# TensorE's order between search and attention written by hand, search counts queued behind chosen evictions, and a third staging buffer for weights

## The chip, the cores and the metric

The kernel runs on one core of one Trainium2 chip. The metric is device time of one execution in microseconds (us). Five engines work side by side, each through its own instructions in a fixed order: TensorE (PE in the profile, with PEld for its weight loads), VectorE (DVE), ScalarE (ACT), GpSimd (POOL) and SyncE (SP), which here only issues DMA transfers. An engine whose next instruction has to wait holds up everything behind it.

## The reference

Two layers (DEPTH = 2) over 1024 positions of width 1024, in float32. Cut to what matters:

```
for l in range(DEPTH):
    h = rmsnorm(x, g_pre[l]) * (1 + scale) + shift
    p = h @ w_in[l]
    u_val, u_gate, g_conv, c_q, c_kv, k_idx, w_idx, g_attn = split(p)
    y_conv = conformer_conv(u_val, u_gate, ...) * silu(g_conv)
    y_attn = dsa_attention(c_q, c_kv, k_idx, w_idx, ...) * silu(g_attn)
    y = concatenate([y_conv, y_attn]) @ w_out[l]
    x = x + gate * rmsnorm(y, g_post[l])

conformer_conv: a = u_val * sigmoid(u_gate); causal depthwise conv, width 31;
                layernorm over 512 channels; silu; @ w_pw2
dsa_attention:  score[t, s] = sum_h w[t, h] * relu(q_idx[t, h] . k_idx[s])
                keep the 256 best keys of each query (causal), add a relative bias,
                softmax over them, times the latent values (8 heads), @ w_uv
```

## The kernel before

The work of a layer runs in five parts: latents (the narrow columns of `w_in`), the indexer (the scores), a **middle**, the attention, and the output projection. Every float32 product that needs precision is three TensorE products of a high and a low half (`mm3`, lines 85 to 89), so matrices are first split by `load_w` (line 91): a DMA brings a third of the matrix into a staging tile `raw` (two such buffers), ScalarE writes the high half (line 107), GpSimd or VectorE the low half (line 108).

The middle is what the change rewrites. It holds six kinds of work.

- `u_proj` (line 583): eight blocks of 48 products of 512 columns, for the two inputs of the convolution. Blocks 1 to 3 are spread between the index products by `tc.issue_after(marks[...])`; blocks 4 to 7 follow them. VectorE evicts every second block (line 601), and a finished pair goes to DRAM (`ad`, line 603).
- `conv` (line 606): eight blocks `c_block(q)`. Each reads back a rearranged piece of `ad` into `at` (line 616, pieces of 128 bytes), loads four weight tiles `wt` of 512 KB (line 626; five buffers of tag `t4`), makes 32 small products (64 instructions in the trace), and is evicted by VectorE into `An` (line 637).
- `gate_proj` (line 677): eight projections of 48 products, whose results ScalarE evicts through Silu (line 688), four into `yc` and four into `ya`.
- `conv_norm` (line 644): layer norm of `An` by `bn_stats` and `bn_aggr` on VectorE, two tiny products and 32 scalings (line 671).
- `pw2` (line 704): for each of four position groups `zt` transposes, Silu on ScalarE, a split into `silh` and `sill`, 48 products `pw`, and four multiplications into `yc` on VectorE (`gated`, line 738).
- `topk` (line 472): a bitwise binary search for each query's 256th best score, 15 and then 16 steps. Each step counts, in six score tiles of 384 to 1024 columns, how many scores lie below a candidate: three tiles on VectorE (line 528), three on ScalarE (line 525), and GpSimd makes the next candidate. Then, tile by tile, the kept keys are marked (lines 570 to 580, the **selection**).

Attention (line 753) goes over four pairs of heads and, in each, over four chunks of 256 queries, c = 0 to 3 (the last pair in the order 3, 1, 2, 0). Chunk c needs the selection of score tiles 2c-2 and 2c-1 only, chunk 0 needs none. `split` (line 854) then splits `yc` and `ya` for the output projection.

The order is a planner's: the program text gives priorities, a simulated time line picks what each engine runs next, and the result is a fixed order per engine. `EARLY`, `STEPS` and the calls in lines 983 to 1034 set the text's order. SP's transfers are ordered the same way, so one that waits for its data holds up those behind it.

## Time and profile before

| | |
|---|---|
| median of 3 runs | 1253.68 us (1253.31 to 1253.84) |
| the profiled execution | 1254.51 us, of which 1252.8 us is its span |
| TensorE busy / mean granted clock | 1188.3 us (95%) / 0.983 |
| VectorE, ScalarE, GpSimd busy | 915.3, 688.1, 628.0 us |
| DMA | 128.10 MB, mean 102 GB/s |

The stage tables below give, for a stretch of the span, the busy time of each engine, then the granted TensorE clock as a share of full speed, the share of time in which the DMA engines were busy, and GB/s. A stretch of TensorE at clock 0.50 runs its products at half speed. A busy TensorE is not proof of full speed, since the ends of pipelined products are modelled; idle time of it is real.

### The profile page before, as it was taken

Reading aid. Unit: us, or ns where it says so; the run is one execution under the profiler, and the core shown is the slowest. Engines: PE = TensorE matmul, PEld = TensorE weight load, DVE = VectorE, ACT = ScalarE, POOL = GpSimd, SP = SyncE. Lnnn points to the kernel's source line nnn. Section 1 sums busy time; section 2 is a strip of 40 time slices with the busy share of each in tenths; the row PEclk is TensorE's granted clock in tenths of the full one; section 3 lists DMA queues with packets and bytes.
Section 4 is the critical chain, followed back from the end, with each engine's and each line's share of the span. In section 5 each row is a group of like instructions: output and inputs, shape, how many; then the busy total and the mean of one; then the engine's idle time right before and its main releaser. Section 6 shows DMA issues by size and latency. Waiting matters only on the chain. (4 is left out here: it accounts for less than half of the span.)

```text
span 1252.8 us, 23059 instructions
## 1 busy us (share of the span) xinstructions
PE 1188.3 (95%) x7832; PEld 974.9 (78%) x7832; DVE 915.3 (73%) x2239; ACT 688.1 (55%) x1580; POOL 628.0 (50%) x1222
## 2 busy tenths in 40 slices
PE   6999999898998999999999999989979899999998
PEld 3888888557886777789988888866768677777998
DVE  3667899999777667757686579989985866677214
ACT  3645768667626556522355466877682465564221
POOL 3441146447536457855585202554673465588222
PEclk9999999899999999999999999989989899999999
DMA  9411266771010000137751123767111100012215
GB/s 360 144 51 34 52 206 209 243 250 52 11 43 21 9 9 26 52 108 267 241 202 53 44 51 107 233 209 211 55 32 28 34 10 5 5 54 74 74 35 185
DMA packets 90854, 128.10 MB, mean 102 GB/s; under 512 B 41320, under 2 KB 68464, under 8 KB 90736
## 3 DMA queue, kind: packets, MB, share of 16 engines
q1 hardware_dynamic: 90736, 126.63, 31.6%
q8 instruction: 62, 1.02, 0.3%
q14 instruction: 56, 0.46, 0.1%
HBM read 114.01 MB, written 12.59 MB: 101 GB/s over the span
## 5 line engine op out<-in xcount | busy, mean ns | idle before, releaser
L528 DVE TENSOR_SCALAR_CACHE_REDUCE jv<-pl,cand 128x768 int16<-128x768 uint16 (+1 forms) x186 | 187.8, 1009 | 17.7 <-DVE jv L528 6.6
L525 ACT ACTIVATE ja<-pl,cand 128x896 int8<-128x896 uint16 (+1 forms) x186 | 153.8, 827 | 40.6 <-POOL cand L535 34.8
L803 ACT ACTIVATE p<-p,mx 128x128 f32<-128x128 f32 (+7 forms) x128 | 98.8, 772 | 55.1 <-DVE mx L800 53.1
L805 POOL TENSOR_SCALAR p<-p,ri 128x128 f32<-128x128 f32 (+7 forms) x128 | 99.8, 784 | 43.8 <-DVE ri L804 43.5
L108 POOL TENSOR_TENSOR wul<-raw,wuh 128x342 fp32r<-128x342 f32 (+1 forms) x48 | 48.6, 1022 | 132.1 <-ACT wuh L107 116.9
L89 PE MATMUL o<-woh,yl 128*128 128x256 f32 x384 | 108.7, 283 | 2.1 <-POOL yl L861 2.1
L87 PE MATMUL o<-woh,yh 128*128 128x256 f32 x384 | 109.4, 286 | 0.5 <-DVE yrr L903 0.5
L88 PE MATMUL o<-wol,yh 128*128 128x256 f32 x384 | 108.5, 283 | 0.0
L87 PE MATMUL g<-hT,wgh 128*128 128x512 f32 x256 | 103.3, 404 | 2.6 <-ACT ya L688 2.2
L89 PE MATMUL g<-hT,wgl 128*128 128x512 f32 x256 | 102.3, 399 | 0.0
L88 PE MATMUL g<-hT,wgh 128*128 128x512 f32 x256 | 101.6, 397 | 0.0
L87 PE MATMUL u<-hT,wuh 128*128 128x512 f32 x256 | 100.8, 394 | 0.0
L88 PE MATMUL u<-hT,wuh 128*128 128x512 f32 x256 | 100.0, 391 | 0.0
L89 PE MATMUL u<-hT,wul 128*128 128x512 f32 x256 | 99.9, 390 | 0.0
L817 PE MATMUL pt<-ident,p 128*128 128x128 f32 x576 | 94.6, 278 | 2.4 <-ACT pt L822 1.7
L790 POOL TENSOR_TENSOR p<-tb,score 128x256 f32<-128x256 f32 x96 | 71.2, 749 | 48.2 <-PE pt L817 46.1
L843 PE MATMUL av<-pt,v 128*64 128x256 f32 (+1 forms) x640 | 93.3, 368 | 0.0
L461 DVE SCALAR_TENSOR_TENSOR score<-relu,widx,score 128x384 f32<-128x384 f32 (+2 forms) x84 | 79.2, 976 | 18.4 <-ACT relu L453 17.5
L817 PEld LDWEIGHTS pt<-ident,p 128*128 128x128 f32 x576 | 67.4, 140 | 25.5 <-issue 10.9
L822 ACT ACTIVATE pt<-pt 128x512 f32<-128x512 f32 (+2 forms) x96 | 50.2, 523 | 64.4 <-PE pt L817 63.8
L453 ACT ACTIVATE relu<-ixs 128x512 f32<-128x512 f32 (+2 forms) x140 | 66.4, 522 | 34.5 <-PE ixs L447 34.1
L447 PE MATMUL ixs<-ix 128*128 128x512 f32 (+2 forms) x320 | 76.3, 356 | 0.4 <-DVE ix L436 0.4
(302 smaller groups left out, 3463.6 us busy)
## 6 DMA issues: line engine op xcount, KB each, us to landing
wt<-in_wl_dram SPq DMA_DIRECT2D x64, 512.0 KB, 5.1
wa<-in_w_mod_dram SPq DMA_DIRECT2D x32, 512.0 KB, 5.2
raw<-in_w_in_dram SPq DMA_DIRECT2D x64, 171.0 KB, 2.5
wa<-in_w_ada_dram SPq DMA_DIRECT2D x16, 512.0 KB, 9.8
raw<-in_w_out_dram SPq DMA_DIRECT2D x32, 171.0 KB, 2.4
raw<-in_w_in_dram SPq DMA_DIRECT2D x32, 170.0 KB, 2.6
ad<-A SPq DMA_DIRECT2D x8, 512.0 KB, 3.3
at<-ad SPq DMA_DIRECT2D x16, 256.0 KB, 6.5
```

What stands on the lines that cost most here:

```text
L87: T.matmul(o, ah, bh, start=first, stop=False)
L88: T.matmul(o, ah, bl, start=False, stop=False)
L89: return T.matmul(o, al, bh, start=False, stop=last)
L447: mark = T.matmul(o[:, :c1 - c0], s_[:, 128 * i:128 * i + 128], ix[:, kk, c0:c1], start=kk == 0, stop=kk == 1)
L461: V.scalar_tensor_tensor(acc, r[:, :w], wc, acc, op0=OP.mult, op1=OP.add)
L525: S.activation(ja[:, :wid(j)], src, AF.Sign, scale=-1.0, bias=col(cand, c), accum_out=col(ct_, c))
L528: V.tensor_scalar(jv[:, :wid(j)], src, col(cand, c), None, op0=OP.is_lt, op1=OP.add, accum_out=col(ct_, c))
L790: G.tensor_tensor(nb, tb, sc[:, OFF[i] + n0:OFF[i] + w], op=OP.add)
L803: mark[0] = S.activation(p[:, :w], p[:, :w], AF.Exp, scale=-1.0, bias=m[:, 2:3], accum_out=ri[:, 0:1])
L805: mark[1] = G.tensor_scalar(p[:, :w], p[:, :w], ri[:, 1:2], 1.0, op0=OP.mult, op1=OP.mult)
L817: T.transpose(t[:, 128 * j:128 * j + 128], p[:, 128 * (j0 + j):128 * (j0 + j) + 128], ident)
L843: T.matmul(o[64 * e:64 * e + 64, t0:256], lh, pts[e][j // 4][:, j % 4, t0:256], start=j == 0, stop=j == 2 * c + 1)
```

## The change

TensorE's instructions from u block 4 to `v_proj` stand in program order (`tc.manual_schedule(engines={T.engine})`). The text of that order is new: generators yield after 12 or 24 products, a convolution block comes after every 36 products of u blocks 4 to 7 and gates 0 and 1, and the transposes and Silu of `pw2` (`prepared`) stand one or two gate halves ahead of its products. The four `wt` loads of a block are issued ahead of the preceding block's end, and the store to `ad` is queued behind the last issued `wt` load.

`Pace` keeps two clocks while the program is written: TensorE's assumed time (2.8 us for 12 products of u, 2.1 us for a convolution block, and so on) with a list of VectorE's evictions and when they fall due, and VectorE's own free time. Each count of the search on VectorE is queued behind the last eviction that would be due by then.

The other parts: `raw` has three buffers; `bn_aggr` is replaced by a few operations over all 32 tiles; the bias tile `tb` is made once (`near_bias`, 8 operations after the first indexer, stored to DRAM as `td`) and not in each head of each layer; `ya` takes the memory of `An`; the second half of `w_uq` loads into `w4` buffers and not into the search's `pl` tile; `w_uv` into half-size `f` tiles; the count's unused output is int8; the selection of the two widest tiles moves into the attention's first head pair, behind chunks 0 and 1; the split of `yc` moves into the last head pair, its high half to ScalarE; and the first group of the output projection takes its rows in the order in which the attention ends.

```diff
-    BUFS = {"t4": 5, "f": 3, "raw": 2, ...
+    BUFS = {"t4": 5, "f": 3, "raw": 3, ...
+class Pace:
+    def pe(self, us):
+        self.t += us
+    def op(self, r, us, lag=0.5):
+        self.events.append((self.t + lag, r.ins, us))
+        return r
+    def start(self, at):
+        self.free, self.last, self.i = at, None, 0
+    def count(self, us):
+        while self.i < len(self.events) and self.events[self.i][0] <= self.free:
+            _, self.last, d = self.events[self.i]
+            self.free += d
+            self.i += 1
+        self.free += us
+        return self.last
...
-                            V.tensor_scalar(jv[:, :wid(j)], src, col(cand, c), None, op0=OP.is_lt,
-                                            op1=OP.add, accum_out=col(ct_, c))
+                            after = pace[0].count(0.0013 * wid(j) + 0.12)
+                            with tc.issue_after(after) if after is not None else nullcontext():
+                                V.tensor_scalar(jv[:, :wid(j)], src, col(cand, c), None, op0=OP.is_lt,
+                                                op1=OP.add, accum_out=col(ct_, c))
...
-            if which:
-                nc.sync.dma_start(ad[cb], A[:, cb, :])
+                if which and half:
+                    with tc.issue_after(wt_dma[0].ins) if wt_dma[0] is not None else nullcontext():
+                        nc.sync.dma_start(ad[cb], A[:, cb, :])
...
         for t in range(32):
-            V.bn_stats(bs[:, t], An[:, t])
-            V.bn_aggr(mv[:, t, :], bs[:, t])
+            pace[0].op(V.bn_stats(bs[:, t], An[:, t]), 0.28)
+        V.tensor_tensor(me, bs[:, :, 1], bs[:, :, 4], op=OP.add)
+        V.tensor_tensor(d, bs[:, :, 1], bs[:, :, 4], op=OP.subtract)
+        V.tensor_tensor(va, bs[:, :, 2], bs[:, :, 5], op=OP.add)
+        V.tensor_tensor(d, d, d, op=OP.mult)
+        V.scalar_tensor_tensor(d, d, 32.0, va, op0=OP.mult, op1=OP.add)
...
+                if pr == 0 and at < 2:
+                    select(4 + at)
+                elif pr == 3 and at < 3:
+                    with tc.issue_after(late[0][-1]), tc.issue_after(late[1][-1]):
+                        if at == 0:
+                            ys = Split(yc, ["hp"] * 4)
+                        for n in range(3 * at, min(3 * at + 3, 8)):
+                            ys.part(n // 2, 512 * (n % 2), 512, V)
...
+        ya = An.rearrange("p (k t) c -> p k (t c)", k=4)
+        pace[0] = Pace()
+        with tc.manual_schedule(engines={T.engine}):
+            cs = [c_block(q) for q in range(8)]
...
+            def conv_products():
+                q = next(due)
+                next(cs[q])
+                if q < 7:
+                    next(cs[q + 1])
...
+            next(cs[0])
+            quarters = 0
+            for i in range(4, 10):
+                if i == 8:
+                    steps = mod_gate(lg_ps("mod")) if l == 0 else iter(())
+                    yc = st("r16", [P, 4, 1024], name="yc")
+                    load_gate(0)
+                    load_gate(1)
+                block = u_block(i // 2, i % 2) if i < 8 else gw[i - 8]
+                for n in range(4 if i < 8 else 6):
+                    next(block)
+                    if i >= 8 and n % 3 == 2:
+                        continue
+                    quarters += 1
+                    if quarters % 3 == 0:
+                        conv_products()
+            load_gate(2)
+            load_gate(3)
+            norm = conv_norm(An)
+            next(norm)
+            gate(2)
+            gate(2, 1)
+            gate(3, 2)
+            next(norm)
+            load_gate(4)
+            gate(3, 2)
+            next(norm)
+            prepared, products = pw2(l, An, yc)
+            gate(4, 2, True)
+            sil = [prepared(0)]
+            next(gw[4])
+            gate(4)
...
+            gate(5, 0, True)
+            sil.append(prepared(1))
+            next(gw[5])
+            products(0, sil[0])
+            gate(5)
...
+            wq = [load_w(w_uq[l, :, 0:1024], 1024, "wuq", "w4", eng=V)]
+            wv = load_w(w_uv[l], 512, "wv", "f")
+            next(gw[7])
+            products(3, sil[3])
+            wq.append(load_w(w_uq[l, :, 1024:2048], 1024, "wuq", "w4", eng=V))
+            next(gw[7])
+            next(gw[7])
+            v = v_proj(l, kv, wv)
+        select = topk(l, sc)
+        for j in range(4):
+            select(j)
+        w0, ys = attention(l, cq, kv, v, sc, ya, wq, select, yc)
```

More of the change, by code (lines that the diff above doesn't have):

```diff
@@ L111, in hybrid_kernel @@
     MOD = {}
+    wt_dma = [None]
+    pace = [None]
     UNITS = ["hq"] * 6 + ["hv"] * 2 + ["hp"] * 6 + ["hv"] * 2
@@ L155, in hybrid_kernel, with near_bias @@
     ad = dr.tile([4, P, 1024], F32, name="ad")
+    td = dr.tile([H, P, 256], F32, name="td")
+    def near_bias():
+        for h in range(H):
+            tb = st("t5", [P, 256], name="tb")
+            nc.sync.dma_start(tb, t5[:, h, :])
+            V.tensor_scalar(tb, tb, -1.0, far[:, h:h + 1], op0=OP.mult, op1=OP.add)
+            nc.sync.dma_start(td[h], tb)
     def mod_setup(l):
@@ L549, in by_group @@
             return r
+        pace[0].start(12.0)
         hi = search(pl, by_group(thr, "thg"), 15)
@@ L560, in topk @@
         V.tensor_tensor(thr, thr, cnt, op=OP.add)
+        pace[0].free += 13.0
         lo = search(pl.bitcast(U16), by_group(thr, "thg"), 16)
@@ L613, in block @@
         def block(q):
+            ws = []
+            for gg in range(4):
+                ws.append(st("t4", [P, 4, 4, 64], name="wt"))
+                wt_dma[0] = nc.sync.dma_start(ws[gg], wl[l, 4 * q + gg].rearrange("p (c e v) -> p c e v", c=4, e=4))
+            yield
             at = st("f", [P, 16, 33], name="at")
@@ L710, in pw2, with prepared @@
         ycv = yc.rearrange("p c (b t) -> p c t b", t=32)
-        def products(tg):
-            acc = [lg_ps("pw") for _ in range(2)]
+        def prepared(tg):
             hi = st("t4", [P, 4, 256], FR, name="silh")
@@ L725, in products @@
                 bs = slice(128 * hb, 128 * hb + 128)
-                V.tensor_copy(hi[:, :, bs], f)
+                pace[0].op(V.tensor_copy(hi[:, :, bs], f), 0.45, 5.0)
                 G.tensor_tensor(lo[:, :, bs], f, f32(hi[:, :, bs]), op=OP.subtract)
+            pace[0].pe(0.8)
+            return hi, lo
+        def products(tg, sil):
+            hi, lo = sil
+            acc = [lg_ps("pw") for _ in range(2)]
             for e in range(4):
@@ L732, in products @@
                         (hi[:, e], lo[:, e]), e + cp % 2 == 0, e == 3 and cp % 2 == 1)
-            return acc
+            pace[0].pe(5.8)
+            gated(tg, acc)
         def gated(tg, acc):
@@ L737, in gated @@
                 yv = ycv[:, cp, 8 * tg:8 * tg + 8, :]
-                V.tensor_tensor(yv, acc[cp // 2][:, 256 * (cp % 2):256 * (cp % 2) + 256]
-                                .rearrange("p (t b) -> p t b", t=8), yv, op=OP.mult)
-        return products, gated
+                pace[0].op(V.tensor_tensor(yv, acc[cp // 2][:, 256 * (cp % 2):256 * (cp % 2) + 256]
+                                           .rearrange("p (t b) -> p t b", t=8), yv, op=OP.mult), 0.68)
+        return prepared, products
     def v_proj(l, kv, w):
@@ L808, in attention @@
         turn = [0]
+        late = [[], []]
         mark = [None, None]
@@ L1028, in hybrid_kernel @@
-        for _ in steps:
-            pass
-        topk(l, sc)
-        dump(f"sel{l}", sc)
-        wq.append(load_w(w_uq[l, :, 1024:2048], 1024, "wuq", "pl", eng=V))
-        v = v_proj(l, kv, wv)
-        w0 = attention(l, cq, kv, v, sc, ya, wq)
-        dump(f"ya{l}", ya)
-        yT = split(yc, ["hp"] * 4) + split(ya, ["hp", "hp", "hv", "hv"])
+        for i in range(1, 4):
+            for _ in u_block(i // 2, i % 2):
+                pass
+        ya = An.rearrange("p (k t) c -> p k (t c)", k=4)
@@ new lines, in hybrid_kernel, with load_gate, gate @@
+        pace[0] = Pace()
+        with tc.manual_schedule(engines={T.engine}):
+            cs = [c_block(q) for q in range(8)]
+            due = iter(range(8))
+            yc, gw, steps = None, {}, iter(())
+            def conv_products():
[3 more added lines that the diff above has]
+                    next(cs[q + 1])
+            def load_gate(g):
+                gw[g] = gate_proj(u, gate_w(l, g // 4, g % 4), g % 4, ya if g > 3 else yc, g == 7)
+            def gate(g, n=0, held=False):
+                for _ in range(2 if held else 3):
+                    next(gw[g])
+                for _ in range(n):
+                    if next(steps, 0) is None:
+                        pace[0].pe(0.8)
+            next(cs[0])
[25 more added lines that the diff above has]
+            next(norm)
+            dump(f"A{l}", An)
+            prepared, products = pw2(l, An, yc)
[3 more added lines that the diff above has]
+            gate(4)
+            for _ in steps:
+                pass
+            load_gate(5)
+            gate(5, 0, True)
[3 more added lines that the diff above has]
+            gate(5)
+            load_gate(6)
+            gate(6, 0, True)
+            sil.append(prepared(2))
+            next(gw[6])
+            products(1, sil[1])
+            load_gate(7)
+            gate(6)
+            sil.append(prepared(3))
+            products(2, sil[2])
+            wq = [load_w(w_uq[l, :, 0:1024], 1024, "wuq", "w4", eng=V)]
[5 more added lines that the diff above has]
+            next(gw[7])
+            dump(f"yc{l}", yc)
+            v = v_proj(l, kv, wv)
```

217 lines of the change are left out of this document (87 added, 130 removed).

## The prediction

> **What bounds the kernel now.** I read the page first: TensorE is busy for 95% of the span, so the whole kernel can lose only what TensorE stands idle or runs slowly. Then I cut the two middles into stages and read, per stage, the length, TensorE's busy time (first number after the length), VectorE's (third), then granted clock, DMA share and GB/s.
>
> ```profile
> 167.40:217.20 49.80, 49.80 (x385) 40.66 (x383) 46.14 (x93) 40.36 (x90) 29.42 (x107) 1.00 0.77 239
> 217.20:262.50 45.30, 38.63 (x421) 27.28 (x420) 41.48 (x83) 32.01 (x65) 21.56 (x86) 0.89 0.76 245
> 262.50:300.00 37.50, 35.92 (x201) 24.88 (x198) 35.83 (x140) 22.83 (x52) 24.45 (x60) 1.00 0.42 145
> 300.00:345.00 45.00, 39.15 (x246) 34.85 (x245) 34.40 (x74) 31.57 (x78) 28.05 (x79) 0.96 0.08 23
> 345.00:397.00 52.00, 47.29 (x232) 38.40 (x231) 39.82 (x79) 22.73 (x48) 23.13 (x25) 0.97 0.14 38
> 397.00:527.00 130.00, 129.28 (x816) 95.87 (x812) 91.60 (x345) 75.99 (x166) 86.54 (x115) 1.00 0.09 23
> 776.90:826.00 49.10, 49.10 (x383) 40.25 (x382) 45.76 (x93) 40.02 (x88) 28.72 (x103) 1.00 0.76 239
> 826.00:870.00 44.00, 37.11 (x406) 26.59 (x404) 40.32 (x79) 31.62 (x64) 21.46 (x85) 0.92 0.77 239
> 870.00:905.00 35.00, 33.49 (x163) 25.44 (x156) 33.23 (x124) 25.26 (x60) 21.28 (x61) 1.00 0.18 50
> 905.00:945.00 40.00, 30.65 (x187) 27.34 (x186) 35.19 (x82) 28.93 (x72) 29.27 (x76) 0.87 0.09 25
> 945.00:1001.00 56.00, 51.82 (x253) 43.40 (x252) 38.82 (x64) 20.49 (x38) 22.42 (x23) 0.94 0.12 35
> ```
>
> Length minus busy is idle time. Attention (397 to 527) has 0.7 us of it and nothing to give. The middles have it in three places: the end of the convolution (6.67 and 6.89 us), norm and pw2 (1.58 + 5.85, 1.51 + 9.35), and the entry to attention (4.71 and 4.18): 40.7 us in all. Where TensorE stood idle, its clock then fell to half. The same view cut to the half-clock stretches:
>
> ```profile
> 228.00:238.00 10.00, 6.18 (x54) 3.65 (x55) 8.07 (x19) 5.78 (x12) 4.58 (x21) 0.50 0.99 300
> 310.00:313.00 3.00, 3.00 (x16) 3.00 (x15) 2.24 (x5) 2.31 (x6) 2.67 (x7) 0.50 0.12 21
> 378.10:381.40 3.30, 3.13 (x7) 2.48 (x8) 3.30 (x4) 1.64 (x4) 2.68 (x2) 0.50 0.00 0
> 838.90:845.60 6.70, 3.95 (x36) 2.49 (x37) 4.77 (x12) 2.59 (x7) 3.12 (x18) 0.50 1.00 346
> 914.00:924.00 10.00, 7.49 (x32) 6.70 (x33) 8.12 (x17) 9.81 (x26) 7.99 (x19) 0.50 0.22 60
> 989.00:995.60 6.60, 5.87 (x17) 4.28 (x16) 5.04 (x7) 3.69 (x6) 4.64 (x5) 0.50 0.18 53
> ```
>
> Half of the busy time in them is lost: (6.18 + 3.95)/2 = 5.1 us at the convolution, (3.00 + 7.49)/2 = 5.2 at norm and pw2, (3.13 + 5.87)/2 = 4.5 at the entry. With the idle time the three places cost **18.6, 23.5 and 13.4 us**, together 55.5.
>
> **Part by part.** *Convolution.* Four rows of the time line (PE, DVE, SP, SP, PE) tell how its stall arose in layer 0.
>
> ```profile
> 216.98 0.39 PE L89 MATMUL u<-hT,wul 128*128 128x512 f32 x1
> ```
> ```profile
> 225.88 0.68 DVE L601 SCALAR_TENSOR_TENSOR A<-A,u 128x512 f32<-128x512 f32 x1
> ```
> ```profile
> 226.59 0.33 SPq L603 DMA_DIRECT2D ad<-A  x1
> 227.01 1.69 SPq L626 DMA_DIRECT2D wt<-in_wl_dram  x3
> ```
> ```profile
> 231.82 1.08 PE L633 MATMUL cv<-wt,at 128*32 128x128 f32 x16 [5.85 <-DMA wt<-in_wl_dram]
> ```
>
> The last u product ends at 217.4. Its eviction runs at 225.9, since counts stand ahead of it in VectorE's order; the store of `ad` waits for it at the head of SP's queue; the `wt` loads behind it go out at 227.0; TensorE waits 5.85 us. The change cuts this chain twice: counts go behind the eviction, and the store goes behind the `wt` loads. The new wait of the store holds up, on SP, the `at` of its own pair and the `raw` loads behind; `at` is needed five quarters of 12 products later, and a third `raw` buffer covers the loads. Of 18.6 us I keep 1 per layer for late weights (bounds: nothing, and rival A): gain 16.6.
>
> Whole blocks also break the product stream less often. Leaving a convolution group costs 0.10 us: the starts below are 0.34 apart, then 0.24.
>
> ```profile
> 225.00 0.50 PE L89 MATMUL g<-hT,wgl 128*128 128x512 f32 x1
> 225.34 0.40 PE L87 MATMUL g<-hT,wgh 128*128 128x512 f32 x1
> 225.58 0.40 PE L88 MATMUL g<-hT,wgh 128*128 128x512 f32 x1
> ```
>
> At most 32 groups a layer (one per `wt`) become 8, so between 0 and 2 x 24 x 0.10 = 4.8 us; I take 1.5, as much of the convolution already runs in longer groups.
>
> *Norm and pw2.* TensorE waits there for VectorE's scalings, ScalarE's Silu and the split, with nothing in between. The new order puts three gate halves between the statistics and the first norm product, and a gate half or more, 24 x 0.24 = 5.8 us, between each `prepared` and its products. The longest of these waits is 2.9 us (quoted below), so a half covers any one. I keep 1 per layer: gain 21.5. Replacing `bn_aggr` is off TensorE's path and counts as 0; it gives VectorE time.
>
> *Entry to attention.* The chain before: VectorE waits for pw products that come late, so the selection and the low half of `w_uq` behind it come late, so the staging buffers stay taken and the `w_uq` loads stand 24.9 us at SP, and the queries wait (DVE, SP, PE rows).
>
> ```profile
> 349.87 1.24 DVE L738 TENSOR_TENSOR yc<-pw,yc 128x256 f32<-128x256 f32 x2 [9.37 <-PE pw L89]
> ```
> ```profile
> 349.97 24.89 SPq L106 DMA_DIRECT2D raw<-in_w_uq_dram  x6
> ```
> ```profile
> 378.27 0.79 PE L87 MATMUL uq<-cq,wuqh 128*128 128x512 f32 x1 [3.26 <-ACT ya L688]
> ```
>
> Afterwards the gated multiplications stand inside the gates, `w_uq` has its own buffers, and only four of six tiles must be selected first. What is late next is the selection of the last two, which chunk 3 of the first pair needs. The selection's operations on VectorE (six tiles), and the removed `bn_aggr`, in layer 0:
>
> ```profile
> L577 DVE TENSOR_TENSOR_SCAN score<-eq 128x384 f32<-128x384 f32 (+5 forms) x6 | 10.9, 1828 | 0.0
> L572 DVE TENSOR_SCALAR_CACHE_REDUCE gt<-score,tf 128x384 f32<-128x384 f32 (+5 forms) x6 | 5.6, 939 | 0.0
> L578 DVE SCALAR_TENSOR_TENSOR eq<-score,need,eq 128x384 f32<-128x384 f32 (+5 forms) x6 | 5.6, 942 | 0.0
> L576 DVE TENSOR_SCALAR eq<-score,tf 128x384 f32<-128x384 f32 (+5 forms) x6 | 4.5, 747 | 0.9 <-POOL gt L579 0.9
> L652 DVE BATCH_NORM_AGGREGATE lns<-lns 128x2 f32<-128x6 f32 x32 | 4.2, 157 | 0.0
> ```
>
> 26.6 us for 4224 columns; the last two tiles have 1920, so 12.1 us move into attention. Chunks 0 to 2 are 21 of a pair's 36 blocks: 130/4 x 21/36 = 19.0 us of TensorE, in which VectorE already has 91.6/130 x 19.0 = 13.4. With 12.1 that is 25.5, 6.5 too much. The next queries and the next pair's first chunks may fill the hole. Bounds: 0, and 6.5 plus a half-clock stretch; I keep 5 per layer, 3.3 idle and 1.7 for the clock: gain 13.4 - 10 = 3.4.
>
> The 1.7 rests on the rows: the clock was down from 914 although no gap before it was longer than 2.9 us.
>
> ```profile
> 911.77 0.66 PE L719 MATMUL zt<-ident,An 128*128 128x128 f32 x4 [2.86 <-DVE lns L669]
> 914.65 1.11 PE L719 MATMUL zt<-ident,An 128*128 128x128 f32 x4 [2.22 <-ACT sl L723]
> ```
>
> The Trainium skill ("TensorE: Matmul & The Clock Gate", section "Why this matters for your kernels") ties the half clock to idle gaps over about 3 us. By that rule gaps of 3.3 us or less in pieces would cost only their length, and the sum would be 3.4 us lower, 1205; the trace speaks against it here.
>
> *End of attention.* The first output products wait 1.1 us in each layer for the split; the new row order and the earlier split of `yc` end that: 2.2 us at most, of which I take all.
>
> ```profile
> PE o L89 <- POOL yl L861: 1.1, 1, 1.1
> ```
>
> The split's casts move to ScalarE, busy for 76 of 130 us there; cost 0, at worst the 1.1 us stay.
>
> *VectorE's cover.* Everything above assumes that the search ends in time. Layer 0, 167 to 397: VectorE 197.7 us busy, minus 4.2 and 12.1 makes 181.4; TensorE 210.8, minus 6.2 of half clock, makes 204.6. Layer 1: 193.3 - 16.3 = 177.0 against 202.2 - 8.7 = 193.5. So VectorE has 23 and 16.5 us to spare, in which the eight `near_bias` operations (16 leave attention) cost nothing. No row shows a VectorE count with int8 output:
>
> ```profile
> L528 DVE TENSOR_SCALAR_CACHE_REDUCE jv<-pl,cand 128x768 int16<-128x768 uint16 (+1 forms) x186 | 187.8, 1009 | 17.7 <-DVE jv L528 6.6
> ```
>
> 93 counts a layer, 94 us: 10% either way is 9 us, inside the slack; I take 0.
>
> **Sum.** 16.6 + 1.5 + 21.5 + 3.4 + 2.2 = 45.2 us. The profiled execution took 1254.5, so 1209.3; it stood 0.8 above the median, so **1208.5**.
>
> **Rivals.**
> *A, slower: the weights set the convolution's pace.* 36 products x 0.24 = 8.6 us and a block, 16 instructions in 1.08 at half clock, so 64 in 2.2, make 10.8 us. In it must come four `wt`, one `at`, half an `ad` and 3/4 of a weight matrix: 2.10 + 0.26 + 0.26 + 0.39 = 3.0 MB, 279 GB/s.
>
> ```profile
> wt<-in_wl_dram SPq DMA_DIRECT2D x64, 512.0 KB, 5.1
> ...
> at<-ad SPq DMA_DIRECT2D x16, 256.0 KB, 6.5
> ```
>
> Against it: with the DMA engines full the rows show 300 and 346 GB/s. For it: over the convolution's stages only 239 to 245 were reached, and the five `wt` buffers come free during the preceding block. At 239 a block takes 12.6, 1.8 more; 16 blocks: +29, 1237. If each wait also brings a half-clock stretch of 3.3 us (1.6 lost), +26 more: 1263, slower than before. It decides at 45.2/16 = 2.8 us lost per block. Everything in TensorE's order stands behind a late block. The Trainium skill ("DMA: Bandwidth & Descriptors", section "Specifications") puts full rate at transfers of 512 B and more; `at` comes in pieces of 128. If that doubled its weight, a block would need 302 GB/s and at 300 lose 0.1 us; the `at` row agrees that it is slow for its size.
>
> *B: the search is held up.* Each count now waits for evictions that may come late; behind it wait the other counts, GpSimd's candidates and ScalarE's counts. 4 u, 8 convolution and 16 gated evictions a layer, each 1 us late, make 28 us, 5 and 11.5 over the slack; with two half-clock stretches +20: 1228. For it: the 9.37 us row above. Against it: the idle time ahead of all counts was 17.7 us in both layers together (the count's row).
>
> *C: the order by hand takes all.* Nothing of the 14 us kept back stays: 1194.5.
>
> *D: it doesn't do what it says.* Only TensorE's order is by hand; ScalarE, GpSimd and most of VectorE stay in the planner's, so norm and pw2 keep their waits: 1230.
>
> **How the numbers follow.** Forecast, 1199 to 1220: 0.49. C 0.16, B 0.11, D 0.08, A without the clock 0.07, A with it 0.09. The range, 1194 to 1236, leaves out A with the clock, half of A without, and the low end of C, 0.17 or so. A measurement can tell 0.2% from no change. Faster: 0.49 + 0.16 + 0.11 + 0.08 + 0.07 = 0.91; of A with the clock 0.02 falls within 0.2%, 0.07 is slower.
>
> **What would show it.** Right: no PE wait for `wt` over 1 us and the store of `ad` within 3 us of the last u product; no half clock from 230 to 330; pw and zt waits under 1 us; the search over before TensorE leaves the gates; in the first head pair a wait of TensorE for the selection. Wrong: `wt` waits in every block (A); VectorE idle ahead of counts for evictions and a late selection (B); the old zt and pw waits (D). The forecast fails upward if the first pair's chunk 3 waits much longer than 5 us, since nothing in before shows that place.

## The result, and the profile after

The changed kernel takes **1234.2 us** (median of 4 runs, 1233.3 to 1235.5) where the kernel before takes 1253.5: ratio 0.985, 95% interval 0.983 to 0.986. So it is faster, clear of the noise, but by 19 us and 1.5%, not by the 45 us that were forecast. The profiled execution's span went from 1252.8 to 1232.2 us.

The same stages as before, read from the changed kernel's windows (length, then busy time of TensorE, weight loads, VectorE, ScalarE, GpSimd, then granted clock, DMA share, GB/s). The first seven rows are layer 0, the others layer 1:

```profile
168.80:220.00 51.20, 51.20 (x502) 41.72 (x500) 44.77 (x91) 39.17 (x85) 29.33 (x103) 1.00 0.88 280
220.00:262.00 42.00, 42.00 (x354) 34.12 (x356) 37.12 (x98) 25.14 (x51) 18.39 (x65) 1.00 0.81 266
262.00:300.00 38.00, 36.40 (x219) 27.60 (x212) 32.16 (x87) 26.57 (x64) 29.57 (x66) 1.00 0.35 104
300.00:350.00 50.00, 50.00 (x314) 45.20 (x313) 42.72 (x88) 40.59 (x98) 27.20 (x87) 1.00 0.14 39
350.00:375.00 25.00, 17.56 (x74) 14.28 (x74) 21.70 (x50) 14.15 (x28) 13.39 (x24) 0.84 0.00 1
375.00:400.00 25.00, 19.78 (x98) 13.77 (x97) 22.49 (x65) 11.34 (x24) 19.95 (x21) 0.88 0.00 1
400.00:517.40 117.40, 116.59 (x740) 85.99 (x739) 78.00 (x303) 70.30 (x154) 74.10 (x102) 1.00 0.09 26
768.20:820.00 51.80, 51.80 (x504) 42.22 (x503) 45.35 (x93) 39.43 (x86) 29.74 (x105) 1.00 0.87 279
820.00:862.00 42.00, 42.00 (x351) 34.37 (x350) 37.12 (x98) 25.46 (x50) 18.03 (x63) 1.00 0.62 200
862.00:900.00 38.00, 36.40 (x194) 31.12 (x193) 31.77 (x83) 25.95 (x65) 27.85 (x59) 1.00 0.19 56
900.00:950.00 50.00, 50.00 (x298) 44.41 (x297) 43.92 (x89) 40.95 (x98) 28.65 (x95) 1.00 0.13 38
950.00:975.00 25.00, 10.88 (x45) 7.69 (x43) 22.26 (x42) 11.79 (x23) 11.27 (x22) 0.72 0.00 0
975.00:1000.00 25.00, 21.32 (x91) 14.77 (x92) 20.95 (x61) 11.06 (x26) 19.33 (x19) 0.73 0.00 1
1000.00:1119.80 119.80, 118.84 (x751) 88.22 (x751) 80.63 (x313) 71.67 (x156) 76.54 (x104) 1.00 0.09 25
```

From the last index products to the end of the gates (168.8 to 350; in layer 1 the gates end at 944.8, inside the row that ends at 950) TensorE now stands idle for 1.6 us a layer, at full clock throughout. Everything that is left sits in the 50 us behind: idle 7.44 + 5.22 and 14.12 + 3.68 = 30.5 us, and by the clock column 17.56 x 0.16 + 19.78 x 0.12 + 10.88 x 0.28 + 21.32 x 0.27 = 14.0 more. The entry to attention costs **44.5 us where it cost 13.4**. The waits of TensorE over the whole kernel (us in total, times, longest) say for whom:

```profile
PE lg L112 <- DVE mx L847: 18.2, 7, 9.4
PE xt L326 <- DVE xt L992: 9.1, 1, 9.1
PE pt L865 <- POOL p L852: 7.7, 5, 3.1
PE cp L112 <- DVE hT L330: 4.1, 2, 2.4
PE zt L760 <- ACT sl L764: 3.2, 2, 1.6
PE uq L112 <- DVE q L812: 1.9, 2, 1.0
```

No wait for `wt` and none of `pw` is left; `lg` (the logits) waits for VectorE, which has not yet taken the minimum of earlier logits (`mx`). VectorE's time line in layer 0 (start, duration; the last column is idle time and its releaser) shows what it does instead:

```profile
350.20 1.28 DVE L559 TENSOR_SCALAR_CACHE_REDUCE jv<-pl,cand 128x1024 int8<-128x1024 uint16 x1
...
353.38 0.61 DVE L608 TENSOR_SCALAR_CACHE_REDUCE gt<-score,tf 128x384 f32<-128x384 f32 x1
...
366.89 0.28 DVE L847 CUSTOM_DVE_ANT_0 p<-lg,p 128x128 f32<-128x128 f32 x1
...
367.76 2.52 DVE L613 TENSOR_TENSOR_SCAN score<-eq 128x768 f32<-128x768 f32 x1
...
391.78 1.27 DVE L614 SCALAR_TENSOR_TENSOR eq<-score,need,eq 128x1024 f32<-128x1024 f32 x1
```

The search's last count ends at 351.5, 1 us after the last gate product (350.4). From 353.4 to 366.9 VectorE does selection, three evictions of queries and a little else; only then comes the first minimum of chunk 0, whose logits were complete at 359.5. The selection's last operation ends at 393.1.

And one cut of the same view in two, at the last count, for both kernels. Before:

```profile
176.90:335.60 158.70, 144.60 (x1151) 111.58 (x1150) 145.19 (x355) 120.35 (x270) 94.03 (x313) 0.96 0.53 168
335.60:397.00 61.40, 56.69 (x283) 46.60 (x283) 43.27 (x89) 24.39 (x51) 27.38 (x34) 0.97 0.12 32
```

After (layer 0, then layer 1):

```profile
179.90:351.50 171.60, 170.00 (x1283) 140.79 (x1282) 148.74 (x340) 126.43 (x286) 99.82 (x314) 1.00 0.52 165
351.50:393.10 41.60, 29.55 (x128) 22.07 (x126) 36.89 (x90) 20.41 (x42) 25.37 (x31) 0.84 0.00 1
...
951.10:993.50 42.40, 25.23 (x89) 17.18 (x90) 37.29 (x86) 17.86 (x39) 23.37 (x28) 0.68 0.00 0
```

Beside the search TensorE used to do 144.60 x 0.96 = 139 us of work at full speed, and now does 170. The search itself became 12.9 us longer, with only 3.6 us more of VectorE's work in it: VectorE's idle time inside grew from 13.5 to 22.9 us. So TensorE has used up its work when the search ends, and little is left to set beside the selection.

The search consists of two binary searches. Up to the first count of the second one (before, then after):

```profile
176.90:247.10 70.20, 64.35 (x609) 50.04 (x608) 64.01 (x124) 55.19 (x117) 37.70 (x149) 0.93 0.73 226
```
```profile
179.90:262.00 82.10, 82.10 (x749) 66.78 (x751) 72.48 (x165) 57.95 (x124) 41.94 (x154) 1.00 0.84 273
```

So 11.9 of the 12.9 us arise ahead of the second search, which takes 89.5 us where it took 88.5. One part is an exchange: the 32 `bn_stats` (6.3 us) stand between the searches now (255.3 to 261.6) and stood inside the second one before (269.1 to 276.9).

### The profile page after: what moved, and what is told of

Same layout as the page of the kernel before. It is cut to its first block, busy times and chain, and to the rows that moved or that the text cites. A ratio compares the mean times of both kernels' runs of the same rounds, so it can differ in the third digit from the quotient of the medians.

```text
span 1232.2 us, 23069 instructions
## 1 busy us (share of the span) xinstructions
PE 1173.8 (95%) x7832; PEld 975.8 (79%) x7832; DVE 897.0 (73%) x2182; ACT 701.9 (57%) x1616; POOL 606.5 (49%) x1218
## 4 chain that ended last, share of the span: by engine, by line
PE 85%; DVE 5%; POOL 5%; issue 2%; ACT 1%; DMA 1%; SPq 0%; DVEq 0%; POOLq 0%; ACTq 0%
PE av L893 7%; PE pt L865 5%; PE ixs L476 5%; PE u L112 5%; PE u L113 5%; PE u L114 5%; PE g L112 5%; PE g L114 4%; PE g L113 4%; PE o L112 4%; PE o L113 4%; PE o L114 4%; PE lg L112 3%; PE cv L674 2%; PE lg L113 2%; PE lg L114 2%
## 5 line engine op out<-in xcount | busy, mean ns | idle before, releaser
L559 DVE TENSOR_SCALAR_CACHE_REDUCE jv<-pl,cand 128x768 int8<-128x768 uint16 (+1 forms) x186 | 187.9, 1010 | 30.8 <-POOL cand L566 20.0
L112 PE MATMUL g<-hT,wgh 128*128 128x512 f32 x256 | 101.2, 395 | 0.0
L113 PE MATMUL g<-hT,wgh 128*128 128x512 f32 x256 | 99.8, 390 | 0.0
L114 PE MATMUL g<-hT,wgl 128*128 128x512 f32 x256 | 99.7, 389 | 0.0
L837 POOL TENSOR_TENSOR p<-tb,score 128x256 f32<-128x256 f32 x96 | 75.5, 793 | 47.4 <-PE pt L865 47.3
L112 PE MATMUL lg<-kvT,q 128*128 128x384 f32 (+2 forms) x192 | 78.5, 410 | 18.3 <-DVE mx L847 18.2
L966 ACT ACTIVATE ja<-o 128x256 int8<-128x256 f32 x64 | 24.5, 383 | 107.2 <-PE o L114 107.0
```

What stands on the lines that cost most here:

```text
L112: T.matmul(o, ah, bh, start=first, stop=False)
L113: T.matmul(o, ah, bl, start=False, stop=False)
L114: return T.matmul(o, al, bh, start=False, stop=last)
L559: V.tensor_scalar(jv[:, :wid(j)], src, col(cand, c), None, op0=OP.is_lt, op1=OP.add, accum_out=col(ct_, c))
L837: G.tensor_tensor(nb, tb, sc[:, OFF[i] + n0:OFF[i] + w], op=OP.add)
```

## The experiments

Four theories. **1**: VectorE's work up to the selection's end ends last now. **2**: only the selection's place in VectorE's order, ahead of chunk 0, costs. **3**: GpSimd's other work makes the candidates late and the search long. **4**: the queueing of counts makes the search long. All ratios are to the kernel before, which took 1253.3 to 1254.6 us (medians) in these sets of runs; the changed kernel is 1234.2. The intervals are 2 to 3 us to either side, so a difference of 3 to 4 us between two of these runs is little more than the noise.

### The selection without ties, in both kernels

```diff
-            V.tensor_scalar(gt[:, :w], seg(j), col(tf, j), None, op0=OP.is_gt, op1=OP.add,
+            V.tensor_scalar(gt[:, :w], seg(j), col(tf, j), None, op0=OP.is_ge, op1=OP.add,
                             accum_out=col(cnt, j))
-            V.tensor_scalar(col(need, j), col(cnt, j), -1.0, float(TOPK), op0=OP.mult, op1=OP.add)
-            eq = st("t4", [P, 1024], name="eq")
-            V.tensor_scalar(eq[:, :w], seg(j), col(tf, j), None, op0=OP.is_equal)
-            V.tensor_tensor_scan(seg(j), eq[:, :w], eq[:, :w], 0.0, OP.add, OP.max)
-            V.scalar_tensor_tensor(eq[:, :w], seg(j), col(need, j), eq[:, :w], op0=OP.is_le, op1=OP.mult)
-            G.tensor_tensor(gt[:, :w], gt[:, :w], eq[:, :w], op=OP.add)
```

> Selection by one comparison (at or above the threshold) in place of five VectorE operations, a GpSimd sum and the ranking of ties; ties at the threshold are left out of the computation. It takes some 21 us of VectorE's 26.6 us a layer away, all of it behind the end of the search (351 us and 951 us in the changed kernel's trace). Theory 1 (VectorE's work up to and through the selection ends last, TensorE waits for it at the entry to attention): the entry stall shrinks but the search still ends at 351: first logits still wait, 12 to 20 us less in all, 1214 to 1222 us. Theory 2 (only the place of the selection in VectorE's order, ahead of the first chunk's evictions, holds TensorE): the whole stall of 12.7 and 17.8 us with its half clock goes, 35 us or more, below 1200 us. Theory 3 (GpSimd's late candidates make the search late): as theory 1, nothing in the search changes.

Measured: **1199.97 us**, ratio 0.958 (0.956 to 0.960), 34 us below the changed kernel. That is the size that theory 2 named (below 1200), and more than the 12 to 20 us of theory 1; which of them has the cause is settled below, where the selection is moved. The run's windows over the entry in layer 0, with the columns as above:

```profile
350.00:375.00 25.00, 23.51 (x119) 17.92 (x117) 19.14 (x70) 19.49 (x41) 11.96 (x32) 1.00 0.00 1
375.00:400.00 25.00, 24.99 (x155) 19.40 (x154) 15.63 (x59) 14.33 (x30) 12.83 (x18) 1.00 0.04 11
```

Of the 12.7 us idle and 5.2 us of half clock there, 1.5 us idle are left (in layer 1, 3.5 between 930 and 985), and the wait of `lg` for `mx` is gone in both layers, although the search ends no earlier (352.2). So it is not the search's end alone that TensorE waits for, but the work behind it. The same edit in the kernel before:

> The kernel before, with the same edit as the run without ties (21 us a layer less on VectorE in the selection, GpSimd's addition gone; keys that tie with the 256th are all kept). If the selection became the bound only through the change (theory 1), it gains little here, at most the entry's 13.4 us: 1240 to 1254. If the selection was already as costly before, it gains what it gained in the changed kernel, 34 us: 1219 to 1225.

Measured: **1239.78 us**, ratio 0.988 (0.986 to 0.990), 14.8 us below its own runs of before: at the edge of the first expectation (1240) and far from the second. Its windows for the two stages from pw2's end into attention:

```profile
345.00:397.00 52.00, 51.56 (x270) 43.08 (x270) 22.87 (x76) 27.13 (x57) 16.30 (x27) 1.00 0.13 38
...
945.00:1001.00 56.00, 55.56 (x292) 46.59 (x291) 25.54 (x84) 30.05 (x63) 18.12 (x29) 1.00 0.13 36
```

The entry's loss, 13.4 us by the prediction's rows, is gone, and the time fell by about that. The four times make a table:

| | with ties | without |
|---|---|---|
| before | 1253.5 to 1254.5 | 1239.8 |
| after | 1234.2 | 1200.0 |

Without the ties the change is worth 40 us. The forecast for all its terms but the entry was 45.2 - 3.4 = 41.8. So the middle's gains are real, and about half of them are given back to the selection: the part of it that this edit leaves out cost 15 us before and costs 34 now.

### A shorter search

```diff
-            for b in range(bits - 1, -1, -1):
+            for b in range(bits - 1, bits - 1 - (steps or bits), -1):
-        lo = search(pl.bitcast(U16), by_group(thr, "thg"), 16)
+        lo = search(pl.bitcast(U16), by_group(thr, "thg"), 16, 12)
```

> The second search leaves out its last 4 of 16 steps (the threshold's four low bits are not resolved). A step takes VectorE 3.4 us, so the search ends about 13.6 us earlier in each layer, with all else as it was. Theory 1: the entry stall gives nearly all of that back, 20 to 30 us, 1204 to 1214 us. Theory 2: the selection still stands ahead of the first chunk, so TensorE waits as long from its own arrival: at most 8 us, 1226 us or more.

Measured: **1218.1 us**, ratio 0.972 (0.970 to 0.974), 16 us below, between the ranges of theory 1 (1204 to 1214) and theory 2 (1226 or more). The last count ends 22 us earlier in layer 0 (329.4), but the last scan only 4 us (387.4); in layer 1 the last scan ends 14.5 us earlier (977.0 against 991.5), 4 of which layer 0 had brought. VectorE's time line of layer 0 tells why so little is left of 22 us:

```profile
336.60 0.60 DVE L608 TENSOR_SCALAR_CACHE_REDUCE gt<-score,tf 128x384 f32<-128x384 f32 x1
...
343.74 1.36 DVE L133 TENSOR_TENSOR wuql<-raw,wuqh 128x342 fp32r<-128x342 f32 x3 [6.35 <-ACT wuqh L132]
345.50 1.24 DVE L786 TENSOR_TENSOR yc<-pw,yc 128x256 f32<-128x256 f32 x2 [0.39 <-PE pw L114]
346.64 0.43 DVE L612 TENSOR_SCALAR eq<-score,tf 128x384 f32<-128x384 f32 x1
```

The first tile's selection begins at 336.6 and stops for over 9 us behind a weight split and gated products, which stand ahead of its next operation in VectorE's order and wait for ScalarE and TensorE. The time won in the search is partly lost in the queue.

### The counts shared out the other way

```diff
-    ACT_TILES = (0,2,4)
+    ACT_TILES = (1,3,5)
```

> The search's counts are shared out the other way: ScalarE counts the tiles of 512, 768 and 1024 columns, VectorE those of 384, 640 and 896. VectorE has 31 x 384 columns, about 15 us, less to count in each layer, ScalarE 10 us more. If VectorE's work from the search's start to the selection's end is what ends last (theory 1), the search ends 8 us or more earlier and, at the 0.6 that a us of search was worth in the run with the short search, the time falls by 10 to 18 us: 1216 to 1225. If the search's chain through three engines sets its pace, its end stays within 3 us and the time at 1231 to 1237; if ScalarE becomes the bound, above 1238.

Measured: **1231.0 us**, ratio 0.981 (0.979 to 0.983), 3.2 us below. VectorE's counts fell from 187.9 to 163.0 us in the two layers, and in layer 0 they end at 337.1, 14 us earlier; the last scan ends at 391.5, where it ended in the changed kernel (391.1). In layer 1 the search (first to last count of VectorE) is only 4 us shorter (167.6 us against 171.6). VectorE's time line of this run just behind the search:

```profile
340.81 0.89 DVE L596 CAST th<-res 128x6 int16<-128x6 f32 x1
345.53 0.18 DVE L597 CAST th<-res 128x6 uint16<-128x6 f32 x1 [3.82 <-POOL res L570]
```

The threshold is not made by VectorE alone: it waited 3.8 us for GpSimd's result. Both simple readings fall: the time is neither VectorE's sum (24.9 us less of it gave 3.2) nor untouched. The short search took about as much out of VectorE's counts (163.6 us left of 187.9) and gave 16; it left out those steps on ScalarE and GpSimd too, where this run gives ScalarE more.

### No queue for the counts; nothing else for GpSimd; the start values

```diff
-                            with tc.issue_after(after) if after is not None else nullcontext():
+                            with nullcontext():
```

> TensorE's order by hand stays, but no count is queued behind an eviction: the planner places them. Theory 4 (the queueing itself makes the search 13 us longer than before): the search ends up to 13 us earlier, the convolution and norm waits return in part, 1220 to 1235 us. Theory 1: VectorE has the same work before the search's end, and evictions that come late hold TensorE up instead: 1234 to 1250 us, with waits for evictions back in the middle.

Measured: **1230.6 us**, ratio 0.982 (0.980 to 0.985), 3.6 us below the changed kernel, in theory 4's range and below theory 1's (1234 to 1250). The search ends 6 us earlier in both layers (345.2, 945.6), but it also begins earlier: it is 4.9 us shorter in layer 0 (166.7 us) and 1.6 in layer 1 (170.0). In return `zt` waits 4.3 us in all for scalings and `cv` 2.4 for `wt`. The search had grown by 12.9 and 14.7 us, so the queueing, theory 4, explains not much over a third of that in layer 0, a tenth in layer 1, and little of the time.

```diff
-        return load_w(w_in[l, 8 + 4 * gi + cblk], 1024, "wg")
+        return load_w(w_in[l, 8 + 4 * gi + cblk], 1024, "wg", low=False)
```

> Leaves out the low halves of the gate weights: GpSimd doesn't make them and the products of the low half run on the high half (same number of products). If GpSimd's other work is what makes the search's candidates late (20 us of waits on VectorE in the two layers), these waits fall to about 5 us, the search ends some 5 us earlier in each layer, and by what the run with the short search gave for its 27 us (16 us) the time falls to 1222 to 1230. If the candidates are late for another reason (counts that ScalarE or VectorE deliver late), the waits stay above 15 us and the time stays at 1234 within 3.

Measured: **1239.4 us**, ratio 0.988 (0.986 to 0.990): slower than the changed kernel by 5 us, outside both ranges of the expectation. GpSimd had 41 us less to do, yet the counts waited longer for its candidates, since it now waited 68.0 us for ScalarE's counts (27.9 in the changed kernel). The group of VectorE's counts in this run (busy us, mean ns, then idle time ahead of it and what ended that):

```profile
L560 DVE TENSOR_SCALAR_CACHE_REDUCE jv<-pl,cand 128x768 int8<-128x768 uint16 (+1 forms) x186 | 187.9, 1010 | 39.6 <-POOL cand L567 27.8 <-DVE jv L560 3.5 <-ACT ja L555 0.9
```

The same group in the changed kernel:

```profile
L559 DVE TENSOR_SCALAR_CACHE_REDUCE jv<-pl,cand 128x768 int8<-128x768 uint16 (+1 forms) x186 | 187.9, 1010 | 30.8 <-POOL cand L566 20.0 <-DVE jv L559 5.1 <-POOL wgl L133 0.3
```

Theory 3 finds no support here: with less work on GpSimd the search became longer (176.1 us in layer 0), and the candidates waited for counts of another engine. But the planner also ordered ScalarE's work otherwise, so neither the 5 us nor the longer search has a single cause shown, and a run below, which gives GpSimd more to do, points the other way.

```diff
-                V.memset(cand, 2.0 ** (bits - 1) - 0.5)
+                G.memset(cand, 2.0 ** (bits - 1) - 0.5)
```

> One operation moved: the start values of the search's candidates are written by GpSimd and no longer by VectorE, where those of the second search stand behind the 32 bn_stats (6.27 us, in which GpSimd and ScalarE idle for 5.5 and 4.6 us). If this block between the two searches is what made the search longer, the search ends 4 us or more earlier in each layer and the time falls by 4 to 8 us, to 1226 to 1230. If VectorE's amount of work alone sets the search's end, the counts only change places with bn_stats: 1232 to 1236.

Measured: **1235.3 us**, ratio 0.984 (0.983 to 0.986): no change; the last count ended at 353.1. The start values themselves cost nothing. What the block of `bn_stats` costs is not shown: it still stands between the searches (256.1 to 262.4), with VectorE's first count of the second search behind it (262.3).

### Where the selection stands

```diff
-        for j in range(4):
-            select(j)
...
-                if pr == 0 and at < 2:
-                    select(4 + at)
+                if pr == 0 and at < 3:
+                    select(2 * at)
+                    select(2 * at + 1)
```

> The selection of tiles 0 and 1 is written behind chunk 0 of the first pair, that of 2 and 3 behind chunk 1, of 4 and 5 behind chunk 2; nothing else changes. Theory 2: TensorE no longer waits 4.3 and 9.4 us for the first chunk's logits to be evicted, 10 to 15 us gained, 1219 to 1224 us. Theory 1: VectorE's work to the end of the selection is the same, so what chunk 0 gains the later chunks lose: 1230 to 1238 us.

Measured: **1242.3 us**, ratio 0.991 (0.989 to 0.993), 8 us slower, and slower than theory 1 allowed (1238): each chunk's selection stands just ahead of its use, `lg` waits for `mx` ten times, the last scan ends at 408.2. Theory 2 falls, at least for this place: nothing of the selection stands ahead of chunk 0, and the time rose. The opposite, all six tiles ahead of the first pair:

```diff
-        for j in range(4):
+        for j in range(6):
             select(j)
```

> The move of the last two tiles' selection into the attention is undone: all six tiles are selected ahead of the first head pair, everything else stays as changed. If the whole of VectorE's work up to the selection is what ends last (theory 1), it matters little where in that work the two tiles stand: 1230 to 1245 us, with one long TensorE wait of 10 us or more ahead of the first logits in place of several short ones. If the move itself is what costs (rival: the two tiles' 12 us stand ahead of evictions that chunks 0 to 2 need), undoing it gives 5 us or more: below 1229. If the move hides what it was meant to hide, undoing it costs about 2 x 12 us: above 1250.

Measured: **1244.6 us**, ratio 0.993 (0.991 to 0.994), 10 us slower, with 45.6 us of `lg` waiting for `mx`, the longest 22.0, as theory 1 expected (1230 to 1245, one long wait). Moving two tiles was right and gave 10 us, not the 24 of their work.

### More work for TensorE

```diff
+            more = mm_ps("more")
+            for k in range(8):
+                for n in range(6):
+                    T.matmul(more, hT(u, 0, k)[:, 0:128], hT(u, 0, k)[:, 0:512], start=k + n == 0, stop=k + n == 12)
             v = v_proj(l, kv, wv)
```

> The changed kernel with 48 useless products of 128x512 more in each layer, just ahead of the value projection (about 11 us a layer of TensorE's time, output unchanged). If TensorE waits there for VectorE's work in any case (theory 1), the idle time and the half clock of the entry take most of it: 1234 to 1245, and the first logits' waits shrink. If the middle's length counts in full (rival), 1254 to 1260.

Measured: **1245.9 us**, ratio 0.993 (0.991 to 0.994), 0.9 us above theory 1's range and far from the rival's; `lg` waits 3.7 us for `mx` where it waited 18.2. The time line gives the 48 products in layer 0:

```profile
350.37 11.18 PE L1138 MATMUL more<-hT 128*128 128x512 f32 x48
```

22 us of work in two layers cost 11.6: half of it fits into the holes of the entry. That is direct evidence that a shorter middle is worth only part of its length there.

### The selection through Sign, and help for VectorE

The same result another way. ScalarE's copy of the scores becomes their sign against the threshold; the last rank gives the number of equals, so that VectorE's first comparison and GpSimd's addition go.

```diff
-            S.activation(seg(j), seg(j), AF.Copy, scale=col(sg, j))
+            S.activation(seg(j), seg(j), AF.Sign, scale=col(sg, j), bias=col(tf, j), accum_out=col(cnt, j))
...
+            V.tensor_scalar(eq[:, :w], seg(j), 0.0, None, op0=OP.is_equal)
+            V.tensor_tensor_scan(gt[:, :w], eq[:, :w], eq[:, :w], 0.0, OP.add, OP.max)
+            V.tensor_scalar(col(need, j), col(cnt, j), -0.5, float(TOPK - w // 2), op0=OP.mult, op1=OP.add)
+            V.scalar_tensor_tensor(col(need, j), gt[:, w - 1:w], 0.5, col(need, j), op0=OP.mult, op1=OP.add)
+            V.scalar_tensor_tensor(gt[:, :w], gt[:, :w], col(need, j), seg(j), op0=OP.is_le, op1=OP.add)
+            S.activation(seg(j), gt[:, :w], AF.Relu, scale=-BIG, bias=big)
```

> The selection computed another way, with the same result: ScalarE's Sign(score - threshold) takes the place of its copy of the scores and of VectorE's first comparison, one VectorE operation joins rank and sign, and GpSimd's addition goes; VectorE keeps three operations of 384 to 1024 columns per tile (about 21 of 26.6 us a layer), and the chain of one tile has no step on GpSimd. If VectorE's amount of work at the entry decides, 5.6 us a layer go with a half-clock share on top: 1215 to 1223. If the chain through GpSimd decides (its additions stand between the softmax scalings that TensorE waits for), most of what the run without ties gained comes: 1200 to 1212. If neither: above 1228.

Measured: **1227.6 us**, ratio 0.978 (0.977 to 0.980), 6.6 us below the changed kernel: 4.6 us above the first expectation (1223 at most), just under the third (1228) and far from the second. GpSimd's addition was not what counted. Some 11 us of VectorE's work behind the threshold, both layers together, gave 6.6; without ties, 42 us gave 34.

> The selection through Sign, as in the run of that name, and no count queued behind an eviction. If the two gains are independent, this run is 3 to 6 us below the one with Sign alone; if the search's end no longer matters once the selection is short, it is within 2 us of it.

Measured: **1223.6 us**, ratio 0.976 (0.974 to 0.977): 4.0 us below Sign alone, as much as the 3.6 that the missing queue gave by itself, so the two gains add up, within the noise.

> Sign selection, no queued counts, start values by GpSimd, and the low half of the second set of query weights split by GpSimd (about 2.8 us a layer less on VectorE inside the search). If VectorE's work up to the selection's end decides, each us taken from it counts about once: 1212 to 1219. If what is left at the entry is the serial chain of one chunk (logits, minimum, exponential, scaling, transposes), it stays at 1222 to 1225.

Measured: **1224.2 us**, ratio 0.976 (0.974 to 0.977): no gain from taking the `w_uq` split (5.7 us in two layers) out of VectorE's search. But the search did not become shorter: GpSimd needed 10.3 us for the same split, VectorE's counts waited 24.9 us for candidates where they had waited 18.2, and the search took 173.5 us in layer 0 where it took 167.4 in the run before. So this run does not tell what VectorE's us inside the search are worth.

> As the run before, and all evictions of transposes in the first head pair's chunks 0 to 2 go to ScalarE (half of them were VectorE's). ScalarE is busy for 4.2 of 14 us there, VectorE for 12.6. If VectorE's work decides, 2 to 5 us more are gained; if the chain decides, nothing (within 1.5 us) or a loss.

Measured: **1220.5 us**, ratio 0.973 (0.971 to 0.974): 3.7 us gained by taking evictions off VectorE behind the threshold.

> The run with ScalarE's help in the first head pair, and in addition the marks of equal scores come from ScalarE's Square of the sign and no longer from a VectorE comparison (4.5 us a layer). If each us of VectorE's selection work costs 0.6 to 0.8 us, as between the runs so far, 5 to 8 us are gained: 1212 to 1216. If ScalarE, which has taken over Sign, Square and the evictions, is late in its turn: 1219 or more.

Measured: **1224.6 us**, ratio 0.976 (0.974 to 0.978): 4 us lost. `lg` now waits 6.7 us for ScalarE's evictions of queries (5.1 in the run before) and 8.6 us for minima (3.9), the longest wait of each 3.8 us. ScalarE's lateness is one part, but not shown to be the whole.

> As the run before, with the counts shared out the other way. If the two add up: 1200 to 1208. If either already takes the entry's stalls: within 3 us of the better of them.

Measured: **1219.3 us**, ratio 0.971 (0.969 to 0.973): 5.4 us below the run before, and in neither of the two expectations.

> The run with ScalarE's help in the first head pair (1220.5), with the counts shared out the other way and without Square. Square cost 4 us there (ScalarE became late); the other sharing of the counts gave 5 with Square and 3 alone. If the gains add up, 1214 to 1218, the shortest time so far that keeps the ties; if ScalarE, with 10 us more of counts, is late in its turn, 1219 to 1224.

Measured: **1219.0 us**, ratio 0.971 (0.970 to 0.973). That is the edge of the second expectation (1219 to 1224). With the ties kept this is the shortest time reached, equal to the one above, and 15 us below the changed kernel. Sign, no queue, start values by GpSimd, the other sharing of counts, and ScalarE's evictions: the later ones add little. Whether that is because ScalarE fills up (727.3 us busy, against 701.9 in the changed kernel) was not tested.

## Why the prediction was wrong

**The convolution was right, and more.** Of its 18.6 us the prediction kept back 2; all 18.6 went (42.00 of 42.00 busy at clock 1.00). No wait for `wt` is left. The last u product ended at 222.9 and the store of `ad` started at 224.2. Rival A fell by the same rows: 280 GB/s against the 239 at which it would have cost 29 us, so 239 had been what was asked for, not a limit.

**Switching was mis-sized, low.** 1.5 us were taken from bounds of 0 and 4.8. Busy time by clock, summed over the rows quoted for both layers (397 to 527 counted to the same distance from the output projection), fell from 332.8 to 328.4 in layer 0, and by about 5 in layer 1, where the kernel before has this row behind those quoted:

```profile
1001.00:1138.00 137.00, 135.84 (x849) 100.45 (x847) 96.39 (x369) 80.21 (x178) 90.29 (x121) 1.00 0.08 22
```

Some 10 us in all, part of it from products that no longer stand beside a wait; the share of switching alone was not measured.

**Norm and pw2 were right.** 23.5 us lost before, 3.2 after (`zt` for `sl`, 1.6 in each layer): 20.3 gained of 21.5 forecast. Rival D falls with it.

**The entry failed, and with it the forecast.** The step that was wrong is "VectorE's cover": "VectorE has 23 and 16.5 us to spare", from busy times over 167 to 397. The sum was about right (195.0 us busy from 168.8 to the selection's end at 393.1, less 12.1 for the moved tiles: 182.9, forecast 181.4), but the spare time lies where nothing of the selection can use it. Of VectorE's time from the first count to the selection's end in layer 0, 22.9 us are idle inside the search and 4.7 behind it. Inside, it waits for candidates, which wait for other engines' counts; the threshold comes last, and 26.6 us of selection can only start behind it. In the kernel before, that tail lay beside TensorE's late gates and pw2; the change brought 31 us of that work beside the search. From there followed the second error, "I keep 5 per layer": it weighed only the two tiles that were moved (6.5 us at chunk 3), where TensorE stalled at chunks 1 and 2 for minima that stood behind the first four tiles. 10 us were kept back, 44.5 were lost. The sum with the measured terms, 18.6 + 10.0 + 20.3 - 31.1 and the 2.2 of the end, is 20.0, and the span fell by 20.6; all terms are read from the same two traces, so this is bookkeeping and no test. That 1234 lies inside the stated range (to 1236) is luck: its upper part was there for rivals A, B and D, and what happened is none of them.

**"The search over before TensorE leaves the gates"** was the condition that was written down, and it missed: the last count ended 1 us after the last gate product in layer 0 and 6 us after it in layer 1 (951.1 against 944.8). The runs bear out that the loss hangs on VectorE's work from there to the selection's end: less of it gave 34 us (no ties), 6.6 (Sign) and 3.7 (evictions). Inside the search two runs suggest that the steps of the chain through three engines count and not VectorE's share alone: 24.9 us less of VectorE's counts gave 3.2, and 24.3 us less, with those steps gone on all engines, gave 16. As a forecast of amounts theory 1 did poorly: of the seven runs for which it named a range, one (all tiles first) fell inside.

**Rival B** named a held-up search and 1228, but its mechanism, counts that wait for evictions, is worth only 3.6 us. Why the search became 13 us longer stays open for the larger part. The sixteen `yc` evictions that now all fall inside it (9.8 us) can't be the whole: the first comes at 304.9, in the second search, and eight of them fell inside it before. The eight more (4.9 us) took the place of `bn_stats` and `bn_aggr` (11.6 us), and the second search grew by 1.0 us. What grew is the time ahead of the second search, 11.9 us, where `bn_stats` (6.3 us) now stands; without the queue, `bn_stats` stands behind the first count of the second search again, and that time is 74.2 us and not 82.1, but the second search is 3 us longer. Of GpSimd's other work the two runs say opposite things.

**The end of attention** gave its 2.2 us: the wait of `o` for `yl` is gone. Not in the sum was a second wait ahead of the latents, at the start of layer 1 (`cp` for `hT`, 2.4 us; the one in layer 0 takes 1.7 where it took 1.6).

## What to carry to other kernels

Spare time of an engine counts only where the work in question may use it: cut its sum at the event that releases that work (here the threshold), and compare each side with what the other engines still have to do there. Work that TensorE is given earlier is taken from beside something later; before filling a hole, look at what stood beside the work that fills it. A part's price can be tested in both kernels, as here without ties: 15 us before, 34 after, and the difference is what the change gave back.

## What the runs showed of the hardware

- The granted clock fell to half again after short gaps. In layer 1, by windows of 3 us (columns as above), it had come back to 0.80 and fell, although the gaps from 977 to 983 were 0.5 and 1.2 us:

```profile
977.00:980.00 3.00, 2.46 (x9) 1.14 (x8) 3.00 (x9) 0.25 (x1) 2.80 (x4) 0.80 0.01 3
980.00:983.00 3.00, 1.78 (x10) 1.29 (x11) 2.39 (x10) 1.43 (x5) 3.00 (x2) 0.76 0.00 0
983.00:986.00 3.00, 2.87 (x12) 1.76 (x13) 1.39 (x4) 1.53 (x2) 3.00 (x5) 0.50 0.00 0
```

  The rule that the prediction weighed (the Trainium skill, "TensorE: Matmul & The Clock Gate", section "Why this matters for your kernels") ties the half clock to gaps over about 3 us. Here the clock fell without one: the last gap of that length (3.1 us) had ended at 972.3. What in the small gaps sets it off is not shown.

- One comparison took far longer than its size says: `eq` of 640 columns 1.56 us, and of 768 columns 0.61. The two rows of VectorE's time line in the changed kernel:

```profile
361.64 1.56 DVE L612 TENSOR_SCALAR eq<-score,tf 128x640 f32<-128x640 f32 x1 [0.31 <-POOL gt L615]
...
365.56 0.61 DVE L612 TENSOR_SCALAR eq<-score,tf 128x768 f32<-128x768 f32 x1
```

And the row of GpSimd's that ran beside the first of them:

```profile
360.21 2.64 POOL L615 TENSOR_TENSOR gt<-gt,eq 128x384 f32<-128x384 f32 x2 [7.28 <-PE v L114]
```

  Without GpSimd's additions (the Sign run) the scans, which there write another tile, also took 1650 ns on average and not 1800. That the two engines hinder each other is what these rows suggest; it was not tried by itself.

- The int8 output of the counts changed nothing: 1010 ns on average against 1009 with int16.
